# Moving every third low-part subtraction of a two-pass weight split from VectorE to GpSimd

## The chip, the cores and the metric

The kernel runs on one core of one Trainium2 chip. The metric is the device time of one execution in microseconds (us), from the first to the last instruction on that core; lower is better. The kernel before took 2006.34 us, the median of two runs (2005.94 and 2006.73). One further execution was taken by the hardware profiler; all rows shown below come from it.

The five engines are named as in the profile: PE is TensorE's matmul, PEld its weight load, DVE is VectorE, ACT is ScalarE, POOL is GpSimd, and SP is SyncE, whose queue issues most of the DMAs. A line number such as L138 is a line of the kernel.

## The reference

One decoder layer on 256 tokens of width 2048, in float32. Three sub-layers follow one another, and each ends in a residual sum and a layer norm:

```
x = layer_norm(alpha*x + 0.5*swiglu(x, ffn1_w_gate, ffn1_w_up, ffn1_w_down), ln1_g, ln1_b)
p = x @ w_in                                   # 2048 x 6432
mix = concat(diff_attn_group(p[:, :3072]), rwkv7_group(p[:, 3072:])) @ w_out
x = layer_norm(alpha*x + mix, ln2_g, ln2_b)
x = layer_norm(alpha*x + 0.5*swiglu(x, ffn2_w_gate, ffn2_w_up, ffn2_w_down), ln3_g, ln3_b)

swiglu(x, wg, wu, wd) = (silu(x @ wg) * (x @ wu)) @ wd       # 2048 -> 5632 -> 2048
```

The change touches only the two `swiglu` sub-layers (FFN1 and FFN2). Their three weight matrices of 2048 x 5632 each are read once, in float32.

## The kernel before, in words

**Two-part products.** Every weight and every activation is split into a high part in the type float32r and a low part, the rest. A product is then three matmuls into the same PSUM accumulator: high x high (L113), high activation x low weight (L114), low activation x high weight (L115). The activations are the stationary operand (128 x 128), the weights the moving one (128 x 512).

**One stream of weight pairs.** All big matmuls come from one object, `Stream`. Its method `block` goes through the rows of a weight matrix two 128-row tiles at a time; I call these two tiles a *pair*. `self.step` counts the pairs of the whole kernel from 1. A block of gate or up columns (512 wide) has 8 pairs, a block of down columns 12 or 10. FFN1 therefore has 2 x 11 x 8 + 4 x 12 + 4 x 10 = 264 pairs (1 to 264), the mixer 136 (265 to 400), FFN2 again 264 (401 to 664).

For each pair the code does this:

1. It issues on SP's queue the DMA of the pair, 128 x 1024 float32, into a `raw` tile (L134). There are `NRAW = 3` such buffers, used in turn.
2. ACT rounds it to the high part `wh` (L137).
3. DVE subtracts, `wl = raw - wh` (L138).
4. PE runs 6 matmuls of the pair for the first 128 tokens (`mm(st, 0)`), and 6 for the second 128 tokens of an earlier pair (`mm(..., 1)`), which is `LAG = 4` pairs behind in the FFNs; the lag grows from 0 over the first 20 pairs of the kernel.

The `wh`/`wl` tiles exist in 7 slots in the FFNs, used in turn. A slot is free again when the lagging matmuls have read it. A `raw` buffer is free again when both the rounding and the subtraction have read it, and SP's queue issues the loads in order.

**What sets the order.** Each engine carries out its own instruction list strictly in order. The lists are laid out beforehand by the framework's planner, which plays the program through with its own costs, takes what is ready, and prefers what comes earlier in the program. Semaphores then keep the data dependencies, whatever the real times are.

**What else GpSimd has on its list.** In both FFNs: one-column copies that hold back a later DMA until a certain tile exists (L205, L206, L262, L279), the DMA issues of the layer norm's gain and bias (L207, L208), and the small power for the layer norm (`rs`, L189), which waits for DVE. During FFN1 it also issues the twenty small DMAs of the mixer's tables (L289 to L319).

**What else VectorE does in the FFNs.** `h` (L227), the low part of the transposed hidden tile (L241), the residual sums (L264, L266), statistics (L267) and the layer norm at the end (L193, L194), after which the new activations are split again (L82).

Of the kernel before, what the change touches and what calls it, by code (L numbers as in the profile page):

```python
# [10 lines left out]
F32 = mybir.dt.float32  # L11
F32R = mybir.dt.float32r
AF = mybir.ActivationFunctionType
ALU = mybir.AluOpType
# [24 lines left out]
def build(tc, A, out):  # L39
# [15 lines left out]
    def nm(s):  # L55
        uid[0] += 1
        return f"{s}_{uid[0]}"

    V, SC, G, T = nc.vector, nc.scalar, nc.gpsimd, nc.tensor
# [29 lines left out]
    class Stream:  # L89
# [29 lines left out]
        def block(self, src, c0, w, ks, lhs, done):  # L119
            blk = dict(ks=ks, w=w, lhs=lhs, done=done)  # L120
            for ki in range(0, len(ks), 2):
                for f in self.hooks.get(self.step, ()):
                    f()
                self.step += 1
                n = 2
                r0 = ks[ki][0]
                raw = wp.tile([P, n, NB], F32, tag="raw", name=nm("raw"), bufs=NRAW)
                pool = wp if self.slot < NW["mix"] else self.pool
                wh, wl = (pool.tile([P, n, NB], F32R, tag=f"{t}{self.slot}", name=nm(t)) for t in ("wh", "wl"))
                self.slot = (self.slot + 1) % NW[self.name]  # L130
                g = 1 if self.step == 1 else n
                for k in range(0, n, g):
                    c = slice(k, k + g)
                    nc.sync.dma_start(out=raw[:, c, :w], in_=src[(r0 + k) * P:(r0 + k + g) * P, c0:c0 + w].rearrange("(k p) n -> p k n", p=P))  # L134
                for k in range(0, n, g):
                    c = slice(k, k + g)
                    SC.copy(out=wh[:, c, :w], in_=raw[:, c, :w])  # L137
                    V.tensor_tensor(out=wl[:, c, :w], in0=raw[:, c, :w], in1=wh[:, c, :w].bitcast(F32), op=ALU.subtract)  # L138
                st = (blk, ki, n, wh, wl)
                self.mm(st, 0)  # L140
                self.pend.append(st)
                if len(self.pend) > max(0, min(LAG[self.name], self.step // 4 - 1)):
                    self.mm(self.pend.pop(0), 1)
                self.run_bg()
# [818 lines left out]
```

## Time and profile before

| | |
|---|---|
| median of the runs | 2006.34 us (2005.94 to 2006.73) |
| span of the profiled execution | 2006.8 us |
| PE busy | 1972.1 us, 98% |
| PEld busy | 1618.6 us, 81% |
| DVE busy | 1145.7 us, 57% |
| ACT busy | 885.0 us, 44% |
| POOL busy | 34.2 us, 2% |
| low parts on DVE (L138) | 665 instructions, 807.9 us busy |
| high parts on ACT (L137) | 665 instructions, 694.9 us busy |
| mean granted TensorE clock | 0.990 |

The span runs from the first to the last instruction; the profiled execution has nothing outside it that the runs' times would count, and its 2006.8 us is 0.5 us above their median. Busy shares are averages over the whole span. A group's row gives its busy time, the mean of one instruction in ns, and the idle time of the engine just before its instructions with what ended that idle time. A row of waits gives the total in us, how often, and the longest.

### The profile page before, as it was taken

Reading aid. Unit: us, or ns where it says so; the run is one execution under the profiler, and the core shown is the slowest. Engines: PE = TensorE matmul, PEld = TensorE weight load, DVE = VectorE, ACT = ScalarE, POOL = GpSimd, SP = SyncE. Lnnn points to the kernel's source line nnn. Section 1 sums busy time; section 2 is a strip of 40 time slices with the busy share of each in tenths; the row PEclk is TensorE's granted clock in tenths of the full one; section 3 lists DMA queues with packets and bytes.
Section 4 is the critical chain, followed back from the end, with each engine's and each line's share of the span. In section 5 each row is a group of like instructions: output and inputs, shape, how many; then the busy total and the mean of one; then the engine's idle time right before and its main releaser. Section 6 shows DMA issues by size and latency. Waiting matters only on the chain.

```text
span 2006.8 us, 24924 instructions
## 1 busy us (share of the span) xinstructions
PE 1972.1 (98%) x9671; PEld 1618.6 (81%) x9671; DVE 1145.7 (57%) x1419; ACT 885.0 (44%) x1096; POOL 34.2 (2%) x68
## 2 busy tenths in 40 slices
PE   9999999999999999999999989999999999999997
PEld 7888888888888878878778777788888888888886
DVE  5555554445545566776668777745554544454555
ACT  5444443344444335645565444444444334444432
POOL 0200000000000000000000010000000000000000
PEclk9999999999999999999999989899999999999999
DMA  7766666667666656555445635666666666766663
GB/s 243 220 188 189 187 191 206 211 192 230 190 188 189 195 167 192 155 160 171 137 123 147 187 117 171 210 200 189 189 188 190 206 211 191 230 190 188 190 195 128
DMA packets 202008, 373.35 MB, mean 186 GB/s; under 512 B 22826, under 2 KB 24944, under 8 KB 201120
## 3 DMA queue, kind: packets, MB, share of 16 engines
q1 hardware_dynamic: 182928, 350.53, 57.8%
q10 hardware_dynamic: 17440, 14.29, 2.5%
q0 software_dynamic: 1520, 6.93, 1.0%
q8 instruction: 76, 1.25, 0.3%
q14 instruction: 44, 0.36, 0.0%
HBM read 364.10 MB, written 7.60 MB: 185 GB/s over the span
## 4 chain that ended last, share of the span: by engine, by line
PE 91%; DVE 4%; DMA 2%; ACT 1%; issue 1%; ACTq 0%; POOL 0%; DVEq 0%
PE acc L113 28%; PE acc L115 28%; PE acc L114 28%; DVE wl L138 1%; DMA raw<-in_ffn_w_gate_dram 1%; PE tr L230 1%; ACT wh L137 1%; DVE y L193 1%; DVE y L194 1%; PE sm L556 0%; PE tr L353 0%; DMA raw<-in_ffn_w_up_dram 0%; PE pr L498 0%; PE at L775 0%; PE tr L75 0%
## 5 line engine op out<-in xcount | busy, mean ns | idle before, releaser
L138 DVE TENSOR_TENSOR wl<-raw,wh 128x1024 fp32r<-128x1024 f32 (+1 forms) x665 | 807.9, 1217 | 649.1 <-ACT wh L137 648.4
L137 ACT CAST wh<-raw 128x1024 fp32r<-128x1024 f32 (+1 forms) x665 | 694.9, 1047 | 832.7 <-PE acc L115 728.3
L115 PE MATMUL acc<-wh,xl 128*128 128x512 f32 (+1 forms) x1952 | 740.6, 391 | 0.5 <-DVE xl L82 0.5
L114 PE MATMUL acc<-wl,xh 128*128 128x512 f32 (+1 forms) x1952 | 735.4, 392 | 3.9 <-DVE wl L138 3.9
L113 PE MATMUL acc<-wh,xh 128*128 128x512 f32 (+1 forms) x1952 | 728.1, 392 | 0.3 <-ACT xh L81 0.2
L114 PEld LDWEIGHTS acc<-wl,xh 128*128 128x128 f32 x1952 | 368.0, 189 | 80.0 <-DVE wl L138 5.2
L113 PEld LDWEIGHTS acc<-wh,xh 128*128 128x128 f32 x1952 | 368.2, 189 | 79.1 <-issue 3.0
L115 PEld LDWEIGHTS acc<-wh,xl 128*128 128x128 f32 x1952 | 367.8, 188 | 77.0 <-issue 2.3
L115 PE MATMUL acc<-wh,hh 128*128 128x512 f32 x704 | 254.5, 390 | 0.0
L114 PE MATMUL acc<-wl,hh 128*128 128x512 f32 x704 | 253.6, 389 | 0.0
L113 PE MATMUL acc<-wh,hh 128*128 128x512 f32 x704 | 252.6, 389 | 0.0
L114 PEld LDWEIGHTS acc<-wl,hh 128*128 128x128 f32 x704 | 132.1, 188 | 27.6
L115 PEld LDWEIGHTS acc<-wh,hh 128*128 128x128 f32 x704 | 132.2, 188 | 27.4
L113 PEld LDWEIGHTS acc<-wh,hh 128*128 128x128 f32 x704 | 132.1, 188 | 27.4
L241 DVE TENSOR_TENSOR hh<-tr,hh 128x512 fp32r<-128x512 f32 x44 | 30.4, 691 | 64.2 <-ACT hh L240 64.2
L240 ACT CAST hh<-tr 128x512 fp32r<-128x512 f32 x44 | 25.8, 586 | 91.2 <-PE tr L230 91.2
L227 DVE SCALAR_TENSOR_TENSOR h<-sg,acc 128x512 f32<-128x512 f32 x44 | 30.2, 687 | 34.9 <-PE acc L115 34.9
L222 ACT ACTIVATE sg<-acc 128x512 f32<-128x512 f32 x44 | 26.3, 598 | 42.9 <-PE acc L115 42.9
L230 PEld LDWEIGHTS tr<-ident,h 128*128 128x128 f32 x176 | 21.7, 140 | 6.3 <-DVE h L227 0.7
L230 PE MATMUL tr<-ident,h 128*128 128x128 f32 x176 | 26.4, 272 | 0.3 <-DVE h L227 0.3
L584 DVE TENSOR_TENSOR itmp<-U,Y 64x31 f32<-64x31 f32 (+15 forms) x62 | 20.5, 331 | 7.3 <-DMA U<-dU 5.9
L586 DVE TENSOR_TENSOR Y<-Y,itmp 64x31 f32<-64x31 f32 (+15 forms) x62 | 20.6, 332 | 1.4
(239 smaller groups left out, 746.8 us busy)
## 6 DMA issues: line engine op xcount, KB each, us to landing
raw<-in_ffn_w_up_dram SPq DMA_DIRECT2D x176, 512.0 KB, 3.8
raw<-in_ffn_w_down_dram SPq DMA_DIRECT2D x176, 512.0 KB, 4.2
raw<-in_ffn_w_gate_dram SPq DMA_DIRECT2D x175, 512.0 KB, 3.9
raw<-in_w_in_dram SPq DMA_DIRECT2D x96, 512.0 KB, 3.7
raw<-in_w_out_dram SPq DMA_DIRECT2D x32, 512.0 KB, 4.2
xs<-y ACTq DMA_DIRECT2D x16, 256.0 KB, 3.1
rc<-xs ACTq DMA_DIRECT2D x16, 256.0 KB, 4.3
lng<-in_ln_g_dram POOLq DMA_DIRECT2D x3, 1024.0 KB, 6.5
```

Of the source, the lines that this page charges most:

```text
L113: T.matmul(a, hi, wh[:, j, :w], start=(ki + j == 0), stop=False)
L114: T.matmul(a, hi, wl[:, j, :w], start=False, stop=False)
L115: T.matmul(a, lo, wh[:, j, :w], start=False, stop=(ki + j == last))
L137: SC.copy(out=wh[:, c, :w], in_=raw[:, c, :w])
L138: V.tensor_tensor(out=wl[:, c, :w], in0=raw[:, c, :w], in1=wh[:, c, :w].bitcast(F32), op=ALU.subtract)
L222: SC.activation(out=s, in_=acc, func=AF.Silu)
L227: V.scalar_tensor_tensor(out=h, in0=sg[tt], scalar=0.5, in1=acc, op0=ALU.mult, op1=ALU.mult)
L230: T.transpose(tr[:, i, :], h[:, i * P:(i + 1) * P], ident)
L240: SC.copy(out=hi, in_=tr)
L241: V.tensor_tensor(out=lo, in0=tr, in1=hi.bitcast(F32), op=ALU.subtract)
L584: V.tensor_tensor(out=tv, in0=U[:, 0:j, j:j + 1].to_broadcast([64, j, 32 - j]), in1=Y[:, j:j + 1, j:32].to_broadcast([64, j, 32 - j]), op= ...
L586: V.tensor_tensor(out=Y[:, 0:j, j:32], in0=Y[:, 0:j, j:32], in1=tv, op=ALU.add)
```

## The change

In both FFNs, and only there, a pair whose number leaves the remainder 2 when divided by 3 has its low part subtracted by GpSimd. The others stay on VectorE, as do all pairs of the mixer. The operation, its operands and its place in the program are the same.

```diff
                 for k in range(0, n, g):
                     c = slice(k, k + g)
                     SC.copy(out=wh[:, c, :w], in_=raw[:, c, :w])
-                    V.tensor_tensor(out=wl[:, c, :w], in0=raw[:, c, :w], in1=wh[:, c, :w].bitcast(F32), op=ALU.subtract)
+                    eng = G if self.name == "ffn" and self.step % 3 == 2 else V
+                    eng.tensor_tensor(out=wl[:, c, :w], in0=raw[:, c, :w], in1=wh[:, c, :w].bitcast(F32), op=ALU.subtract)
                 st = (blk, ki, n, wh, wl)
                 self.mm(st, 0)
```

`self.name` is "ffn" in FFN1 and FFN2 and "mix" between them. `V` is `nc.vector`, `G` is `nc.gpsimd`.

## The prediction

> **What bounds the kernel now.** I read the page first, then the waits, then the stages, then one pair's way through its buffers.
>
> ```profile
> span 2006.8 us, 24924 instructions
> ...
> PE 1972.1 (98%) x9671; PEld 1618.6 (81%) x9671; DVE 1145.7 (57%) x1419; ACT 885.0 (44%) x1096; POOL 34.2 (2%) x68
> ...
> PE 91%; DVE 4%; DMA 2%; ACT 1%; issue 1%; ACTq 0%; POOL 0%; DVEq 0%
> ...
> L138 DVE TENSOR_TENSOR wl<-raw,wh 128x1024 fp32r<-128x1024 f32 (+1 forms) x665 | 807.9, 1217 | 649.1 <-ACT wh L137 648.4
> ...
> raw<-in_ffn_w_down_dram SPq DMA_DIRECT2D x176, 512.0 KB, 4.2
> raw<-in_ffn_w_gate_dram SPq DMA_DIRECT2D x175, 512.0 KB, 3.9
> ```
>
> PE is busy 98% of the span and is 91% of the chain that ended last. All that any relief of DVE could win is PE's idle time, 2006.8 - 1972.1 = 34.7 us (1.7%). DVE waits for ACT before the low parts for 648 us: it has room. The waits say how much of PE's idle time the low parts cause:
>
> ```profile
> ACT wh L137 <- PE acc L115: 728.3, 472, 8.2
> ...
> PEld acc L114 <- DVE wl L138: 5.2, 4, 2.5
> ...
> PE acc L114 <- DVE wl L138: 3.9, 3, 2.2
> ```
>
> Seven times in 665 pairs does PE, or its weight load, wait for a low part. The usual wait is the other way round: ACT's rounding waits until PE gives a weight slot back. By stage (columns: length, then PE, PEld, DVE, ACT and POOL busy, clock, DMA share, GB/s):
>
> ```profile
> 0.00:20.00 20.00, 15.40 (x71) 12.30 (x72) 11.38 (x18) 10.15 (x14) 0.70 (x6) 1.00 0.78 266
> 262.00:390.00 128.00, 128.00 (x571) 105.99 (x570) 64.47 (x60) 50.93 (x50) 1.11 (x6) 1.00 0.63 202
> 755.00:1238.00 483.00, 473.65 (x2970) 380.47 (x2969) 343.11 (x638) 260.82 (x445) 11.23 (x12) 0.98 0.53 156
> 1238.00:1265.00 27.00, 23.17 (x93) 18.03 (x92) 24.27 (x35) 10.45 (x12) 1.00 (x1) 0.83 0.59 178
> ```
>
> Inside an FFN (262 to 390 us) PE has no gap at full clock. PE's idle time lies at the start (4.6 us), in the mixer (9.4 us, where nothing is changed) and where FFN2 begins (3.8 us; there DVE is the busier engine); the remaining 17 us are at the two other layer norms, which end an FFN.
>
> Now one pair in that steady stage, from ACT's list:
>
> ```profile
> 325.55 1.05 ACT L137 CAST wh<-raw 128x1024 fp32r<-128x1024 f32 x1 [1.67 <-PE acc L115]
> 328.27 1.05 ACT L137 CAST wh<-raw 128x1024 fp32r<-128x1024 f32 x1 [1.67 <-PE acc L115]
> ```
>
> A pair takes PE 328.27 - 325.55 = 2.72 us, and ACT idles 1.67 us of it. What this room is worth depends on the three raw buffers, so I follow one of them in the chain of waits (start, duration, what):
>
> ```profile
> 40.97 4.71 DMA raw<-in_ffn_w_gate_dram
> ...
> 45.78 1.06 ACT wh L137
> 46.84 0.02 issue
> 46.86 1.24 DVE wl L138
> 48.09 0.02 issue
> 48.11 6.34 DMA raw<-in_ffn_w_gate_dram
> ```
>
> One round of a buffer is load, 0.10 us, rounding 1.06, subtraction 1.24 with its handover, 0.02, and the next load. At a landing of 4.71 that is 48.11 - 40.97 = 7.14 us. Three buffers serve three pairs in a round, so PE lets each round last 3 x 2.72 = 8.16 us. This is the number that the change has to respect. Pair numbers with remainder 2 always meet the same one of three buffers (the count and the buffers both go round in threes), so one buffer carries GpSimd's duration in every round and the others never.
>
> **The change part by part.** *Removed from DVE:* pairs 2, 5, ... 263 and 401, 404, ... 662 are 88 + 88 = 176. At 1.22 us that is 215 us less DVE work, 1146 to about 931 us. Where PE is 100% busy this is worth nothing.
>
> *Added to POOL:* 176 subtractions of 128x1024, which the trace of before does not show on POOL. The nearest rows, from POOL's groups:
>
> ```profile
> L819 POOL TENSOR_TENSOR ars<-vr,neghalf 128x4 f32<-128x4 f32 x8 | 8.2, 1022 | 182.6 <-DVE vr L817 182.6
> L262 POOL COPY rc<-hh 128x1 f32<-128x1 f32 x16 | 2.8, 185 | 679.6 <-DVE y L264 637.0 <-ACT hh L240 42.6
> L596 POOL MEMSET TT<- 128x1024 f32 x2 | 1.9, 953 | 256.2 <-PE pr L479 256.2
> ```
>
> The lower end is one pass over the same shape, 0.95 us. The upper end is three passes (two reads and a write, nothing overlapped) and the fixed cost of the only two-input operation here, 3 x 0.95 + 1.02 = 3.9 us; that one is a power, though, and 0.19 us is what a copy costs. I take two passes, the write beside the reads, and a copy's fixed cost: 2 x 0.95 + 0.19 = 2.1 us, because the memset is the nearest row in shape. POOL's busy time becomes 34 + 176 x 2.1 = about 400 us, off the path.
>
> The Trainium skill speaks against this move: its page "GPSIMD Engine Reference", section "3.1 Elementwise — side-by-side cycle accounting", measures a float32 two-input add of 2048 elements at 4497 ns on GpSimd against 2293 on VectorE and keeps elementwise work on VectorE. By it, half of 4497, 2.25 us (an estimate from that page), would stand in place of my 2.1, and the round below would be 7.9 us in place of 7.8; its VectorE half agrees with the 1.22 us measured here, and no run before this shows the GpSimd half.
>
> *The round in the steady stage.* The raw tile's view for 262 to 390 us, then the loads' views for 390 to 610 and 1590 to 1850:
>
> ```profile
> DMA to landing us min/median/max: 3.5/4.4/5.0
> ```
> ```profile
> DMA to landing us min/median/max: 3.5/4.0/9.1
> ```
> ```profile
> DMA to landing us min/median/max: 3.5/4.4/8.6
> ```
>
> With the slow usual landing: 4.4 + 0.10 + 1.06 + 0.10 (handover to POOL, taken like ACT's) + 2.1 + 0.05 = 7.8 us, under 8.16. So the subtraction may last 8.16 - 5.71 = 2.45 us before PE pays in every round. A later issue of this buffer's load also puts it further behind the load before, so nearer to the 3.5 us end; then up to 3.35 us are free. SP's queue is not held up: the next load waits for DVE's low part a pair later, which ends 2.72 us after the old end of this one. A single late one is covered too. Two pairs (5.44 us) lie between the slot's return and its use, and 1.06 + 0.05 + 1.22 are used of that: 3.1 us spare, of which GpSimd takes 1.0. Steady stages: 0 us. If 2.45 is passed and landings stay, the cost is 176 times the excess.
>
> *Slow landings.* The longest, 8.6 and 9.1 us, already eat the 3.1 us; with 1.0 less to spare, one of them falling on POOL's buffer costs up to 1 us: +1 (0 to +4).
>
> *Start.* Pair 2 is GpSimd's:
>
> ```profile
> 10.13 1.23 DVE L138 TENSOR_TENSOR wl<-raw,wh 128x1024 fp32r<-128x1024 f32 x1 [1.21 <-ACT wh L137]
> 11.27 0.69 DVE L81 CAST xh<-tr 128x512 fp32r<-128x512 f32 x1
> ```
>
> PE waits for everything there; the low part comes 0.9 to 1.0 us later, and the activation split right behind on DVE starts earlier. Until 57 us the round at 4.71 is 8.1, so POOL's buffer no longer catches up: +1 (-0.4 to +4).
>
> *FFN2's begin*, from the chain:
>
> ```profile
> 1248.58 1.23 DVE wl L138
> ...
> 1260.90 1.22 DVE wl L138
> 1262.12 0.04 issue
> 1262.17 0.80 PE acc L114
> ```
>
> The first and the last of these are pairs 401 and 404, both GpSimd's. They leave a chain that runs wholly on DVE: up to -2.4, within the 3.8 us of PE's idle time there; then pairs 407 and 410, loaded with nothing ahead, come 1 us later. The layer norm's power on POOL is queued between them and comes a second after pair 401's. Net -1 (-2.4 to +2). The Trainium skill's "SBUF — State Buffer", section "Who interferes with whom", says that a Vector instruction with two SBUF inputs and a GpSimd instruction that reads SBUF shut each other out for a whole instruction. By that rule up to 2.1 us of the gain here would go back, and nothing in the steady stage, where DVE's next low part starts 2.72 us after POOL's; no row before shows the two together.
>
> *POOL's own list.* The new instructions share it with these (first and last of twenty issues):
>
> ```profile
> 59.13 0.76 POOL L279 COPY sc<-hh 128x1 f32<-128x1 f32 x1 [57.83 <-ACT hh L240]
> 59.84 0.72 POOL L289 DMA_DIRECT2D vr<-in_rwkv_mu_dram  x1
> ...
> 70.41 0.53 POOL L319 DMA_DIRECT2D lq<-in_lambda_k_dram  x1
> ```
>
> Pair 23's high part is ready at about 61.7 us. The planner prefers the earlier pair, so I take one issue, 0.5 us, which the spare hides: 0.
>
> **Sum:** 2006.8 + 0 + 1 + 1 - 1 + 0 = 2007.8, against a median of 2006.34 in the runs; I forecast **2008 us**.
>
> **The rivals.** *The raw round becomes the bound* (slower). At a subtraction of 3.9 us the round is 9.6 us at 4.4 landing and 8.7 at 3.5: 0.5 to 1.4 us too long, 176 times, +90 to +250 us. It decides from 2.45 us (slow landings) to 3.35 (fast ones). For it: the power's 1.02 us. Against it: the memset's 0.95. Chance 0.12.
>
> *The twenty DMA issues go ahead of pair 23.* Its low part then ends at 70.9 + 2.1 = 73.0 and PE, 3.1 us of spare past 63.0, needed it at about 67: +6 us, 2014. For it: the planner put copies for much later work into POOL's idle time. Chance 0.12.
>
> *DVE's relief counts* where DVE leads: -2.4 at FFN2's begin and nothing lost elsewhere, 2004. Chance 0.08.
>
> *No effect by construction* (the condition never true) is excluded: both FFNs set the name, and the count passes every remainder.
>
> **How the numbers follow.** My forecast has 0.68. The low end, 2001, is the relief (-2.4, -0.4) and as much again from a planner's other order in the mixer, whose 9.4 us of idle time can move either way. The high end adds the upper bounds +4, +4, +2, +6 and that 9: 2006.8 + 25 = 2032. This leaves out most of the first rival. A measurement of this kernel can tell about 2% (40 us) from no change. Faster by that is out of reach, since PE's idle time is 34.7 us: 0.01. Slower by it needs 0.23 us of excess in each round, which is nearly all of the first rival: 0.12. The rest, 0.87, is within 2%.
>
> **What would show it.** A GpSimd subtraction of 2 to 2.4 us; DVE near 931 us busy; in the steady stages PE still without gaps, and ACT still waiting for PE, not for DMA, though less before every third pair. Wrong would be: PE waiting for `wl` from POOL in every round; ACT waiting for raw landings there; DVE's own low parts growing longer than 1.22 us; or a block of PE idle time at 67 to 75 us.

## The result, and the profile after

The changed kernel took 2034.47 us (2034.24 to 2034.71), 28 us more than before: ratio 1.0139, 95% interval 1.0109 to 1.0168. By the mark of 2% it is no difference; by the interval it is a loss. The forecast was 2008 us with a range up to 2032. The profiled execution's span is 2032.9 us, 26.1 more than before's 2006.8; its time as a run was 2034.71 us, 1.8 above its span, so spans are compared with spans and times with times below.

First the page of the changed kernel (busy time and instructions of each engine; two groups with busy time, mean ns, idle time before them). All its line numbers from 139 on are one higher than before's.

```profile
span 2032.9 us, 24925 instructions
...
PE 1976.4 (97%) x9671; PEld 1620.1 (80%) x9671; DVE 960.6 (47%) x1243; ACT 885.1 (44%) x1096; POOL 457.2 (22%) x244
...
L139 DVE TENSOR_TENSOR wl<-raw,wh 128x1024 fp32r<-128x1024 f32 (+2 forms) x489 | 616.0, 1262 | 804.2 <-ACT wh L137 793.3
...
L139 POOL TENSOR_TENSOR wl<-raw,wh 128x1024 fp32r<-128x1024 f32 x176 | 423.5, 2407 | 976.8 <-ACT wh L137 974.1
```

The change does what it says: 176 low parts are on POOL, at 2.4 us each. PE's busy time rose by 1976.4 - 1972.1 = 4.3 us and its idle time from 34.7 to 2032.9 - 1976.4 = 56.5 us: of the 26.1 us, 21.8 are new idle time and 4.3 are the same matmuls run more slowly. The waits:

```profile
ACT wh L137 <- PE acc L115: 609.2, 371, 8.4
...
ACT wh L137 <- DMA raw<-in_ffn_w_gate_dram: 69.6, 43, 6.0
ACT wh L137 <- DMA raw<-in_ffn_w_up_dram: 64.5, 49, 5.5
...
ACT wh L137 <- DMA raw<-in_ffn_w_down_dram: 26.0, 29, 2.0
...
PE acc L113 <- ACT sg L223: 7.7, 2, 5.1
```

ACT still waits mostly for PE (728 us before, 609 now), but now 121 times for a raw tile's landing in the FFNs (in the kernel before 37 times for gate and up). That need not cost anything, as the steady stage shows (windows: length, PE, PEld, DVE, ACT and POOL busy, clock, DMA share, GB/s; then ACT's list):

```profile
0.00:20.00 20.00, 15.21 (x70) 11.93 (x71) 9.73 (x16) 9.93 (x13) 3.90 (x8) 1.00 0.79 265
262.00:390.00 128.00, 128.00 (x571) 106.01 (x569) 45.93 (x44) 50.89 (x51) 36.82 (x20) 1.00 0.61 204
```
```profile
326.55 1.06 ACT L137 CAST wh<-raw 128x1024 fp32r<-128x1024 f32 x1 [1.67 <-PE acc L115]
329.27 1.05 ACT L137 CAST wh<-raw 128x1024 fp32r<-128x1024 f32 x1 [1.66 <-PE acc L115]
331.21 1.05 ACT L137 CAST wh<-raw 128x1024 fp32r<-128x1024 f32 x1 [0.89 <-DMA raw<-in_ffn_w_down_dram]
```

Between 262 and 390 us PE has no gap and does the same 571 matmuls as before. ACT's list above shows the rhythm of 2.72 us; the third rounding waits for its landing and still is in time. At the start PE is busy 15.21 of 20 us, 15.40 before. In this stage the landings stayed about as they were; the raw tile's view for 262 to 390 us:

```profile
DMA to landing us min/median/max: 3.5/4.2/5.4
```

(4.4 in the median of the same stage before.) From 390 to 610 us the median rose from 4.0 to 4.4, and over the whole span those of the loads of up, gate and down from 3.8, 3.9 and 4.2 to 4.2, 4.3 and 4.4. The page's chain of waits breaks off in this execution after 1% of the span and says nothing. So the loss lies outside the steady stages. To place it, I compare one row of each layer norm, GpSimd's small power, before and after:

```profile
736.28 1.05 POOL L189 TENSOR_TENSOR rs<-ve,neghalf 128x1 f32<-128x1 f32 x1 [280.74 <-DVE ve L187]
...
1251.71 1.00 POOL L189 TENSOR_TENSOR rs<-ve,neghalf 128x1 f32<-128x1 f32 x1 [48.00 <-DVE ve L187]
...
1990.08 1.02 POOL L189 TENSOR_TENSOR rs<-ve,neghalf 128x1 f32<-128x1 f32 x1 [280.70 <-DVE ve L187]
```
```profile
749.64 1.01 POOL L190 TENSOR_TENSOR rs<-ve,neghalf 128x1 f32<-128x1 f32 x1 [9.40 <-DVE ve L188]
...
1276.46 1.01 POOL L190 TENSOR_TENSOR rs<-ve,neghalf 128x1 f32<-128x1 f32 x1 [50.52 <-DVE ve L188]
...
2016.24 1.00 POOL L190 TENSOR_TENSOR rs<-ve,neghalf 128x1 f32<-128x1 f32 x1 [11.15 <-DVE ve L188]
```

By the first layer norm the changed kernel is 13.4 us late, by the second 24.8, by the third 26.2. The second step, 11.4 us, lies in the mixer, where no instruction was moved. For the first step, here is GpSimd's list (start, duration):

```profile
61.91 0.18 POOL L280 COPY sc<-hh 128x1 f32<-128x1 f32 x1 [2.90 <-ACT hh L241]
62.03 0.74 POOL L290 DMA_DIRECT2D vr<-in_rwkv_mu_dram  x1
...
69.91 0.53 POOL L320 DMA_DIRECT2D lq<-in_lambda_q_dram  x1
70.46 2.51 POOL L139 TENSOR_TENSOR wl<-raw,wh 128x1024 fp32r<-128x1024 f32 x1
```

And ACT's list at the pair whose high part this is, and a little later:

```profile
64.26 1.06 ACT L137 CAST wh<-raw 128x1024 fp32r<-128x1024 f32 x1 [1.46 <-PE acc L115]
...
85.66 2.05 ACT L137 CAST wh<-raw 128x1024 fp32r<-128x1024 f32 x2 [5.50 <-DMA raw<-in_ffn_w_up_dram]
```

The trace holds nineteen table issues, in this kernel and in the one before, and not the twenty of the text ahead of this section. Sixteen of them stand ahead of pair 23's low part, though its high part was ready at 64.26 + 1.06 = 65.3 us. The raw buffers then come back late, ACT waits 5.50 us for a landing with a `sg` behind it on its list, and PE waits 5.08 us for that `sg`.

The same happens once before, on a smaller scale: PE stands for 2.62 us ahead of a matmul at 38.92 us, for the other of the two `sg` in the list of waits. Behind it the clock falls too (columns as above):

```profile
39.90:40.90 1.00, 1.00 (x4) 0.72 (x4) 1.00 (x1) 0.40 (x1) 0.00 (x0) 0.50 1.02 346
```

### The profile page after: what moved, and what is told of

Same layout as the page of the kernel before. It is cut to its first block, busy times and chain, and to the rows that moved or that the text cites. A ratio compares the mean times of both kernels' runs of the same rounds, so it can differ in the third digit from the quotient of the medians.

```text
span 2032.9 us, 24925 instructions
## 1 busy us (share of the span) xinstructions
PE 1976.4 (97%) x9671; PEld 1620.1 (80%) x9671; DVE 960.6 (47%) x1243; ACT 885.1 (44%) x1096; POOL 457.2 (22%) x244
## 3 DMA queue, kind: packets, MB, share of 16 engines
q8 instruction: 76, 1.25, 0.2%
## 5 line engine op out<-in xcount | busy, mean ns | idle before, releaser
L139 DVE TENSOR_TENSOR wl<-raw,wh 128x1024 fp32r<-128x1024 f32 (+2 forms) x489 | 616.0, 1262 | 804.2 <-ACT wh L137 793.3
L139 POOL TENSOR_TENSOR wl<-raw,wh 128x1024 fp32r<-128x1024 f32 x176 | 423.5, 2407 | 976.8 <-ACT wh L137 974.1
L115 PE MATMUL acc<-wh,hh 128*128 128x512 f32 x704 | 257.4, 390 | 0.0
L113 PE MATMUL acc<-wh,hh 128*128 128x512 f32 x704 | 255.3, 389 | 0.0
L820 POOL TENSOR_TENSOR ars<-vr,neghalf 128x4 f32<-128x4 f32 x8 | 8.2, 1023 | 184.8 <-DVE vr L818 146.2
L190 POOL TENSOR_TENSOR rs<-ve,neghalf 128x1 f32<-128x1 f32 x6 | 6.0, 1001 | 95.5 <-DVE ve L188 95.5
```

Source lines behind the costliest of these rows:

```text
L113: T.matmul(a, hi, wh[:, j, :w], start=(ki + j == 0), stop=False)
L115: T.matmul(a, lo, wh[:, j, :w], start=False, stop=(ki + j == last))
L139: eng.tensor_tensor(out=wl[:, c, :w], in0=raw[:, c, :w], in1=wh[:, c, :w].bitcast(F32), op=ALU.subtract)
L190: G.tensor_tensor(out=rs, in0=ve, in1=neghalf, op=ALU.pow)
L820: G.tensor_tensor(out=rs, in0=vr, in1=neghalf[:, :, None].to_broadcast([P, 2, 2]), op=ALU.pow)
```

## The experiments

The suspicion after this comparison was a cause outside the prediction's sum: the planner writes every engine's list by its own clock, and with other durations it wrote other lists. Theory 1 says that these lists are the loss. Theory 2 says that the low part on GpSimd itself is. To separate them, most experiments build the program twice: once with one kernel's choice of engine, to read off each engine's list, and once with the other choice, with ordering edges that force the lists read off (a few places differ still). "Lists of before" below means this. GpSimd's low parts themselves are placed by the planner. A kernel with the forced lists and no moved low part was not run, so the price of the frame itself is not measured apart; what the traces show of it stands under "What stays open".

```
- raw = wp.tile([P, n, NB], F32, tag="raw", name=nm("raw"), bufs=NRAW)
+ raw = wp.tile([P, n, NB], F32, tag=f"raw{self.step % NRAW}", name=nm("raw"))
...
- V.tensor_tensor(out=wl[:, c, :w], ...)
+ eng = G if on_pool and self.name == "ffn" and self.step % 3 == 2 else V
+ eng.tensor_tensor(out=wl[:, c, :w], ...)
...
+ for engine, order in lists.items():
+     mine = [traced[k] for k in order if traced[k].engine == engine]
+     for a, b in zip(mine, mine[1:]):
+         tc.add_manual_dep(b, a.name, info, reason="list of the other kernel")
...
+ _, lists = program(False, None)
+ nc, _ = program(True, lists)
```

**1. All 176 on GpSimd, lists of before.**

> GpSimd subtracts every third pair as in the changed kernel, but each engine's list, and the buffer that each pair gets, is that of the kernel before. Theory 1 (the 28 us come from the other lists that the planner wrote once the durations had changed): 2009 to 2016 us; what stays is 1 to 4 us at the start, 0 to 6 at the twenty table issues (on GpSimd's own list they still lie around pair 23) and 3 to 4 where FFN2 begins. Theory 2 (the GpSimd low part itself, longer than assumed and on a buffer that then comes back late, is the cost): 2026 us or more, since the 176 low parts are all still on GpSimd.

Measured: 2023.73 us; ratio 1.0070 (1.0051 to 1.0089), which is +14 us (10 to 18). Neither theory's range holds it. Half of the loss goes with the lists, half stays.

**2. Lists of the changed kernel, all low parts on VectorE.** The same frame, turned round (and the raw tile as in the changed kernel):

```
- _, lists = program(False, None)
- nc, _ = program(True, lists)
+ _, lists = program(True, None)
+ nc, _ = program(False, lists)
```

> The reverse: the lists are those of the changed kernel on PE, ACT, SP and (but for the 176 low parts) DVE and GpSimd, but VectorE subtracts every pair as before. Theory 1: most of the loss stays without any GpSimd low part, 2018 to 2031 us (the 28 less 3 to 4 for FFN2's begin and less what pair 23's late low part adds). Theory 2: 2004 to 2010 us.

Measured: 2021.77 us; ratio 1.0068 (1.0053 to 1.0083), +14 us (11 to 17), without one low part on GpSimd. Where: the place is the end of the mixer. First before, then this kernel (the last gated RWKV tile on DVE, and the matmul that waits for what follows from it):

```profile
1226.79 1.28 DVE L732 TENSOR_TENSOR og<-BK,sm 128x512 f32<-128x512 f32 x2
```
```profile
1236.76 1.28 DVE L733 TENSOR_TENSOR og<-BK,sm 128x512 f32<-128x512 f32 x2
```
```profile
1238.75 0.80 PE L113 MATMUL acc<-wh,xh 128*128 128x512 f32 x1 [5.25 <-ACT xh L81]
```

The tile comes 10 us later, since the lists interleave the chains of the mixer otherwise, and PE stands for 5.25 us. In its layer-norm rows this kernel is +1.6 us at the first and +12.1 at the second.

**3. Only the steady pairs on GpSimd, lists of before.**

```
- self.step % 3 == 2
+ self.step % 3 == 2 and (28 < self.step < 265 or self.step > 415)
```

> As the kernel with the lists of before, but only pairs 29 to 263 and 416 to 662 (79 + 83 = 162 or so of the 176) go to GpSimd: the start, the table issues and FFN2's begin are VectorE's again. Theory 1, and the prediction's 0 us for the steady stages: 2005 to 2008 us. Theory 2, or a lock between VectorE and GpSimd that costs all along: 2015 us or more.

Measured: 2009.28 us; ratio 1.0005 (0.9996 to 1.0015), +1 us (-1 to +3). It is 1.3 us above the 2005 to 2008 expected, and within the interval 162 of the 176 low parts are free. This is the prediction's 0 for the steady stages, and it leaves the start, the tables and FFN2's begin to cost something.

**4. Without FFN2's begin.** As 1, but pairs 401 to 413 on VectorE (`and not 400 < self.step < 416`).

> As the kernel with the lists of before, but VectorE keeps pairs 401 to 413, the five at FFN2's begin. If VectorE and GpSimd shut each other out there: 3 to 4 us under the kernel with all 176 (the two lengthened layer-norm operations go back from 2.8 to 0.75 us each). If not: within 1 us of it.

Measured: 2017.85 us, 5.9 under experiment 1, more than the 3 to 4 expected. The two profiled executions differ in another place too, the tables, so this run doesn't price the begin by itself; experiment 11 does.

**5. The table issues behind pair 23.** As 1, with two more edges on GpSimd's list:

```
+ tc.add_manual_dep(tables[0], lo_ops[23].name, info, reason="pair 23 first")
+ tc.add_manual_dep(tables[13], lo_ops[26].name, info, reason="pair 26 before the last seven")
```

> All 176 low parts on GpSimd and the lists of the kernel before on the other engines, as in the first pinned kernel (2023.7 us); only GpSimd's own list differs: pair 23's low part stands ahead of all twenty table issues and pair 26's ahead of the last six. If the table issues that stood ahead of pair 23 were the loss between 60 and 100 us (8 us in the first pinned kernel's trace): 2014 to 2018 us, and no idle time of PE at 69 us. If it was GpSimd's later low part as such, or the mere number of things on its list: 2021 us or more.

Measured: 2016.73 us; ratio 1.0040 (1.0025 to 1.0055), 7.0 us under experiment 1. GpSimd's list is now (lines are 3 higher than in the changed kernel):

```profile
61.88 0.58 POOL L283 COPY sc<-hh 128x1 f32<-128x1 f32 x1 [3.08 <-ACT hh L244]
64.50 2.39 POOL L142 TENSOR_TENSOR wl<-raw,wh 128x1024 fp32r<-128x1024 f32 x1 [2.04 <-ACT wh L140]
66.83 0.74 POOL L293 DMA_DIRECT2D vr<-in_rwkv_mu_dram  x1
...
74.52 2.39 POOL L142 TENSOR_TENSOR wl<-raw,wh 128x1024 fp32r<-128x1024 f32 x1 [0.85 <-issue]
```

Pair 23's low part starts at 64.5 us and PE has no idle time there. It was the order on the list, not GpSimd's duration. (With nineteen issues, six stand behind pair 26's low part, whatever the edge's label says.)

**6. Only the steady pairs, lists left to the planner** (the condition of experiment 3 put into the changed kernel).

> The changed kernel with its condition narrowed to pairs 29 to 263 and 416 to 662, the lists left to the planner. With the lists of before these pairs cost nothing (2009.3 us against 2007.7). If the mixer's other lists follow from any change of the durations in the FFN: 2016 to 2021 us, with PE's idle time of about 5 us at the mixer's end, as in the changed kernel. If the start and the table issues brought the other lists about: 2006 to 2010 us.

Measured: 2019.49 us; ratio 1.0055 (1.0040 to 1.0070), +11 us (8 to 14). Moving low parts that cost 1 us by themselves brings the mixer's late tile: by the layer-norm rows +1.9 us at the first, +11.3 at the second. PE stands 5.26 us at the same place as in experiment 2.

**7 and 8. A longer low part.** Experiment 3, but from pair 97 and from pair 425 on (136 pairs) GpSimd subtracts again, half of the tile (`0:1`) or the whole (`c`):

```
+ if eng is G and (96 < self.step < 265 or self.step > 424):
+     G.tensor_tensor(out=wl[:, 0:1, :w], in0=raw[:, 0:1, :w], in1=wh[:, 0:1, :w].bitcast(F32), op=ALU.subtract)
```

> The kernel with the lists of before and pairs 29 to 263 and 416 to 662 on GpSimd (2009.3 us), but for the pairs from 97 on and from 425 on (136 in all) GpSimd subtracts the first half of the low part twice, so that one pair holds its buffer for about 3.6 us in place of 2.40. By the prediction's law for one buffer's round (free up to 2.45 us with slow landings, up to 3.35 with fast ones): 136 times 0.25 to 1.15, so 2043 to 2166 us. If the spare is larger than the law says (a landing that comes sooner the later it is issued): 2009 to 2020 us.

> The same with the whole low part subtracted twice, about 4.8 us a pair. By the prediction's law 136 times 1.45 to 2.35, so 2206 to 2329 us, with ACT waiting for the raw tile's landing in every third pair. If the buffer's round does not bind: under 2060 us.

Measured: 2228.29 us (ratio 1.1083, 1.1057 to 1.1110) and 2378.06 us (1.1821, 1.1787 to 1.1855). Both are above their ranges, because the second operation is longer than I took it to be: with the lengths measured below, the same law gives 2156 to 2278 and 2314 to 2436 us, and both times lie inside. Groups of the half and of the full kernel (busy, mean ns, idle before):

```profile
L142 POOL TENSOR_TENSOR wl<-raw,wh 128x1024 fp32r<-128x1024 f32 x162 | 388.7, 2400 | 897.2 <-ACT wh L140 897.2
L144 POOL TENSOR_TENSOR wl<-raw,wh 128x512 fp32r<-128x512 f32 x136 | 264.7, 1946 | 10.3
```
```profile
L144 POOL TENSOR_TENSOR wl<-raw,wh 128x1024 fp32r<-128x1024 f32 x136 | 422.6, 3107 | 10.4
```

A pair held GpSimd for 2.40 + 10.3/136 + 1.95 = 4.43 us and for 2.40 + 0.08 + 3.11 = 5.59 us. The loss against experiment 3 is 0.1083 x 2007.75 - 1 = 216 us, or 1.59 us a pair, and 0.1821 x 2007.75 - 1 = 365 us, or 2.68. So the subtraction is free up to 4.43 - 1.59 = 2.84 us by the one and 5.59 - 2.68 = 2.91 by the other. This agrees with the law of the buffer's round: the limit lies inside the 2.45 to 3.35 predicted, and the 2.40 us of the change stay under it by 0.4 to 0.5 us. The limit is an estimate, and the round is not isolated by these two runs: the mean clock of the profiled executions was lower too (0.972 and 0.954 against 0.991), VectorE's own low parts between 300 and 600 us took 1.99 and 2.17 us in the median in place of 1.23, and PE waited 91 and 116 times for the second subtraction itself. A run with a fourth raw buffer, which would relieve the round alone, is missing.

**9, 10 and 11. One place at a time.** Lists of before, and on GpSimd only pairs 2 to 20; only 23 and 26; only 401 to 413 (every third each):

```
- self.step % 3 == 2
+ self.step in (2, 5, 8, 11, 14, 17, 20)
```

> The lists of before, and only pairs 2, 5, 8, 11, 14, 17 and 20 on GpSimd. With all 176 the trace is 2 us later by 40 us and no later by 67 us: 2008 to 2011 us against about 2007.5 of the kernel before. The prediction's own term for the start is +1 (-0.4 to +4). If a start without lists of its own costs nothing: within 1 us.

> The lists of before, and only pairs 23 and 26 on GpSimd: 15 of the twenty table issues stand ahead of pair 23's low part. The prediction's rival has 6 us for it; the trace of the kernel with all 176 has 8: 2013 to 2016 us against about 2007.5. If the loss there needs the late buffers of pairs 2 to 20 as well: under 2010 us.

> The lists of before, and only pairs 401, 404, 407, 410 and 413 on GpSimd. If VectorE's layer-norm operations there stand still while GpSimd subtracts (two of them 2 us longer each), and the low parts come 1 us later: 2009 to 2012 us against about 2007.5. By the prediction's own term (-2.4 to +2, taken as -1; VectorE is relieved of two low parts in its chain): 2005 to 2008 us.

Measured, against 2008.02 us for the kernel before: 2010.46 us (ratio 1.0012, 1.0003 to 1.0020), +2.4 us (0.6 to 4.0), as expected; 2011.93 us (1.0021, 1.0012 to 1.0030), +4.2 us (2.4 to 6.0), between the two values expected; 2012.32 us (1.0023, 1.0014 to 1.0031), +4.6 us (2.8 to 6.2), just above the range for a lock, a loss and no gain.

For the tables, the traces of two executions show a dear and a cheap gap. PE's row at the gap and then the window behind it, in experiment 1:

```profile
74.67 0.79 PE L114 MATMUL acc<-wl,xh 128*128 128x512 f32 x1 [5.20 <-POOL wl L139]
```
```profile
75.00:77.00 2.00, 2.00 (x6) 1.52 (x6) 0.00 (x0) 0.00 (x0) 1.98 (x6) 0.50 0.57 121
```

And the same two with pairs 23 and 26 alone:

```profile
69.66 0.50 PE L114 MATMUL acc<-wl,xh 128*128 128x512 f32 x1 [2.31 <-POOL wl L139]
```
```profile
70.00:72.00 2.00, 2.00 (x10) 1.67 (x9) 0.69 (x1) 0.00 (x0) 2.00 (x6) 1.00 0.65 113
```

Behind a gap of 5.20 us PE goes on at a clock of 0.50, 6 matmuls in 2 us in place of 10; behind one of 2.31 it keeps 1.00. That the buffers that come back late from pairs 2 to 20 lengthen the gap in experiment 1 is likely but not shown: experiment 4 has the same low parts there, and in its trace the gap is 3.70 us and the clock stays at 1.00. Part of it is the single execution: the twelve runs of experiment 10 lie between 2009.06 and 2017.38 us, and the one shown, 2009.14, is among the fastest.

For FFN2's begin, the lists of GpSimd, DVE and PE in the kernel with pairs 401 to 413 alone:

```profile
1256.31 2.55 POOL L139 TENSOR_TENSOR wl<-raw,wh 128x1024 fp32r<-128x1024 f32 x1 [2.94 <-ACT wh L137]
...
1256.58 4.16 DVE L195 SCALAR_TENSOR_TENSOR y<-y,rs,lnb 128x512 f32<-128x512 f32 x3
...
1259.46 1.12 PE L75 MATMUL at<-ident,y 128*128 128x128 f32 x4 [5.14 <-DVE y L195]
...
1271.96 0.50 PE L114 MATMUL acc<-wl,xh 128*128 128x512 f32 x1 [2.34 <-POOL wl L139]
```

Pair 401's low part runs on GpSimd from 1256.31 to 1258.86 us, and in that time one of the layer norm's operations on DVE hardly makes headway: three of them take 4.16 us, where the same three took 2.07 in experiment 4:

```profile
1264.42 2.07 DVE L195 SCALAR_TENSOR_TENSOR y<-y,rs,lnb 128x512 f32<-128x512 f32 x3
```

PE's wait for `y` is 5.14 us, in place of 3.04 in the kernel before. Then pair 404's low part comes late and PE waits another 2.34 us.

## Why the prediction was wrong

**The account.** The places priced alone: start 2.4, tables 4.2, steady 1.0, FFN2's begin 4.6, together 12 us; experiment 1 has all four at once, 14. The lists alone cost 14 (experiment 2). 14 + 14 is the 28 us measured. These are sums of figures with 2 to 4 us to either side, so they show the shares and not the last microsecond. By the layer-norm rows of one execution each, the step up to the first is +9.9 us in experiment 1 (lists of before), +1.6 in experiment 2 (lists alone) and +13.4 in the changed kernel; the step from the first to the second +1.6, +10.6 and +11.4; the step from there to the third +4.3, +0.5 and +1.4. So the mixer's loss is that of the lists and most of FFN1's that of the moved low parts; but FFN1 cost the changed kernel more than the two experiments together and FFN2 less, so that the even sum is in part luck.

**The steady stages, 0 us: right**, and for the stated reason (experiments 3, 7, 8). The subtraction was taken as 2.1 us and is 2.40. The estimate worked out from the Trainium skill's page "GPSIMD Engine Reference", section "3.1 Elementwise — side-by-side cycle accounting", 2.25 us, was nearer; the round by it is 5.71 + 2.25 = 7.96, so 8.0 us and not 7.9. The spare, 0.4 to 0.5 us, lies near the lower end of the 0.35 to 1.25 that 2.1 us gave, so the rival of a binding round was closer than it looked, but it did not come true. Of the signs named for it, ACT waiting for raw landings did show in the steady stage (9 of 47 roundings between 262 and 390 us), without cost. *Slow landings*, +1, lies within what experiment 3 measured.

**POOL's own list, "one issue, 0.5 us, which the spare hides: 0": wrong.** "The planner prefers the earlier pair" did not hold: sixteen issues went ahead. This is the rival with chance 0.12, and its mechanism came true as written; its 6 us (7 by its own numbers, since 63.0 + 3.1 is 66.1) are 4.2 alone and 7 among the others. The block of PE idle time named as a sign came later, at 84 us. The rows quoted there spoke for it: the table issues began at 59 us on an idle POOL, and pair 23's high part was ready at 61.7.

**A planner's other order in the mixer: in the range, not in the sum.** This is the step that failed most. The sum took the lists of before as given and put the planner's other order at nothing; only the range let 9 us of mixer idle time "move either way". The lists cost 14 us (experiment 2), and they also came out otherwise, with the same late tile, when only the steady pairs were moved (experiment 6).

**FFN2's begin, -1: wrong in sign.** The relief of DVE's chain by two low parts is not to be seen, and the rows were misread: of the two taken for pairs 401 and 404, the one at 1248.58 us belongs to a pair that VectorE keeps. It is still there in experiment 11, where GpSimd's two come at 1256.31 and 1269.15 us:

```profile
1249.24 1.23 DVE L139 TENSOR_TENSOR wl<-raw,wh 128x1024 fp32r<-128x1024 f32 x1 [1.06 <-ACT wh L137]
```

So one low part, 1.2 us, could leave that chain and not two. The lock was named and priced at "up to 2.1 us of the gain here would go back"; it is 2.1 us on the path, and nothing stood against it. Pair 404's late low part adds the rest.

**The start, +1 (-0.4 to +4): right**, 2.4 measured. **DVE's busy time**, about 931 us: 960.6, mostly since its low parts grew from 1217 to 1262 ns mean, 489 x 0.045 = 22 us, off the path; two lengthened layer-norm operations add 4. The lock was expected to do nothing in the steady stage, but DVE's next low part often fell on GpSimd's: in the whole kernel 53 did, and 45 of them grew. The prediction named this growth as a sign that something is wrong; it was true, and harmless wherever PE had the lead.

**The range's high end, 2032,** added the upper bounds of all terms, 25 us, and was 2.5 us short. Three of its bounds were passed: 14 us for the lists against 9, 7 for the tables (experiment 5) against 6, and 4.6 for FFN2's begin against 2; the start and the steady stages stayed under theirs. The bounds also priced each gap at its own length. Behind a long gap a stretch at half clock can follow, so that a late tile costs more than its lateness; in all, PE's busy time rose by 4.3 us:

```profile
78.00:83.00 5.00, 5.00 (x24) 4.14 (x23) 1.23 (x1) 1.05 (x1) 0.91 (x1) 1.00 0.18 43
89.00:91.00 2.00, 1.95 (x5) 1.56 (x6) 1.70 (x3) 1.49 (x3) 1.19 (x1) 0.50 0.84 221
95.00:98.00 3.00, 3.00 (x15) 2.47 (x14) 1.44 (x2) 2.39 (x3) 0.00 (x0) 1.00 0.34 53
```

In the changed kernel, ahead of the 5.08 us gap at 84 us the clock is 1.00, behind it 0.50, and at 95 us 1.00 again.

**What stays open.** Why the planner's costs lead it to the later order in the mixer was not traced; that the order alone costs this much is shown, its reason is not. The price of the forced lists and of the raw tile's new tag is open too: experiments 9 and 10 move nothing in FFN2, and still their third layer norm comes 1.3 and 1.2 us later behind the second than in the kernel before, with a wait of PE of 0.76 us at about 1269 us for a low part of VectorE, which the kernel before does not have. About 1 us of each price taken in this frame, all of experiment 3's and a part of the begin's 4.6, may be the frame's. A version faster than the kernel before did not show up: the best of the moved ones, experiment 3, equals it.

## What to carry to other kernels

Where a planner writes the instruction lists, a change of engine is two changes, the moved work and the new lists; pin the lists before judging the first, and run the new lists with the old engines to price the second. An engine that looks idle in the busy shares has things on its list: look at what is queued at the hour when the moved work becomes due. A buffer's round, written out as load plus stages against the consumer's pace, gave a range for the limit of the moved step, 2.45 to 3.35 us here, and the two runs that passed it put it at 2.84 and 2.91.

## What the runs showed of the hardware

**VectorE and GpSimd stand still for each other.** The layer norm's second operation (minimum, median, maximum in ns, first before and then after), and in the changed kernel a DVE subtraction with one operand in PSUM, and GpSimd's low parts:

```profile
L194 DVE SCALAR_TENSOR_TENSOR y<-y,rs,lnb x24: 743/747/749, 739.5 to 2001.7; 128x512 f32<-128x512 f32 x24
```
```profile
L195 DVE SCALAR_TENSOR_TENSOR y<-y,rs,lnb x24: 740/744/2832, 752.8 to 2027.8; 128x512 f32<-128x512 f32 x24
...
L242 DVE TENSOR_TENSOR hh<-tr,hh x44: 679/692/693, 61.9 to 1923.5; 128x512 fp32r<-128x512 f32 x44
...
L139 POOL TENSOR_TENSOR wl<-raw,wh x176: 2351/2399/3477, 10.2 to 2002.7; 128x1024 fp32r<-128x1024 f32 x176
```

With both tensor operands in SBUF an operation of 0.75 us grew to 2.83, by 2.1 (the two of the 24 that overlapped a GpSimd subtraction); with one operand in PSUM none of the 44 grew, although eight of them overlapped a GpSimd subtraction. GpSimd's own longest is 3.48 us. The Trainium skill's page "SBUF — State Buffer", section "Who interferes with whom", states just this: a Vector instruction with two SBUF inputs and a GpSimd instruction that reads SBUF exclude each other for a whole instruction, one with a single SBUF input, outside the page's two-port modes, does not. The trace agrees with both halves. That is likely also why the half-tile subtraction of experiment 7 took 1.95 us in the mean: its shortest took 1.26 us, and VectorE's own low parts were longer there as well.

```profile
L144 POOL TENSOR_TENSOR wl<-raw,wh x136: 1257/2126/2335, 274.1 to 2189.9; 128x512 fp32r<-128x512 f32 x136
```

**The clock behind a gap.** Gaps of 5.1 to 5.3 us were followed by some 3 to 6 us at a granted clock of 0.50; the gap of 2.31 us was not, nor was one of 3.70 us in experiment 4. But behind the gap of 2.62 us in the changed kernel and behind the one of 3.04 us in the kernel before, at 1254 us, the clock also fell to 0.50. So in these traces the length of a gap alone does not decide. The Trainium skill's page "TensorE: Matmul & The Clock Gate", section "What's actually happening", puts the fall to half clock at one idle window of about 3.4 us that runs freely. The gaps of over 5 us agree with it, the one of 3.70 us too, which need not hold a whole window; the two of 2.62 and 3.04 us are shorter than that window and still saw the fall, so there the measurement differs from the page, and it decides.
